# Walking a matmul's moving operand backwards, and interleaving the two token tiles of its stationary operand

## The chip, the cores and the metric

The kernel runs on one core of one Trainium2 chip. The metric is the device time of one execution in microseconds (us). The kernel before took 1279.71 us, the median of two runs (1278.69 and 1280.73). The profile is of one execution, whose span from first to last instruction is 1276.7 us.

On TensorE (PE) a matmul has two operands in SBUF. The stationary one, 128 x 128, is loaded into the array by an instruction of its own, which the profile shows on a row called PEld; the moving one is then streamed through the array column by column, up to 512 columns, and the products are summed in a bank of PSUM, 128 x 512 float32.

## The reference

A network of two blocks on 256 tokens of 1024 channels, all in float32: first a block of a state space layer and a causal attention, then two layers that each mix latent attention, a gated convolution and a retention, and end with a feed-forward network. Cut to one such feed-forward step, with the names of the kernel's weights:

```python
h = rms_norm_2(x, ln_ffn_pre)
y = (silu(h @ w_gate) * (h @ w_up)) @ w_down
x = x + rms_norm_2(y, ln_ffn_post)
```

Nearly all of the work is products of that form: 256 rows times a weight matrix of 1024 (or 2816, 512, 256, 128) rows. The change touches how these products are read and written, and nothing of what they compute.

## The kernel before

Every product with a weight matrix is done in three matmuls of a rounded float32 type (float32r in the code). An operand `a` is held as `hi + lo`, where `hi` is `a` rounded to that type and `lo` is what is left over; `x @ w` is then `xh wh + xh wl + xl wh`. The method `mm3` (lines 163 to 167) issues these three, with a block of the activations (128 channels x 128 tokens) as the stationary operand and 512 (a few times 416 or 256) columns of the weights as the moving one.

Weights arrive by `wtile` (line 142) in tiles of 256 rows x 512 columns: one DMA from SyncE's queue into a buffer `raw`, a rounding copy into `hi` on ScalarE (ACT, line 158), and a subtraction into `lo` on VectorE (DVE, line 160). `wbuf` (line 135) hands the buffers out by turns. In the state space layer `hi` and `lo` have four buffers each, in a pool `wp`; for the rest of the program each has six, four in `wp` and two in the stage's own pool `sp`, so that of each six tiles that follow each other four lie in the one place and two in the other. A tile of 2 k-blocks x 2 token tiles gives 12 matmuls.

Activations are made into stationary operands by `split` (line 186), which reads a transposed block out of PSUM (or a temporary), writes the rounded value `dh` on ACT and the remainder `dl` on DVE. `transposed` (line 196) does that for the blocks of one token tile; the pre-norms, the feed-forward, the merge, and the attention outputs all come through it or through `split`. Their pages come from `pages` (line 214): up to four channel blocks, each with its 256 tokens in a row, so that token tile `t` of a block is 128 words that follow each other:

```python
s = slice(t * 128, t * 128 + 128)
self.mm3(pts[t][:, :ncols], xh[:, s], xl[:, s], hi[:, k, :ncols], lo[:, k, :ncols], ...)
```

`gemm` (line 169) computes rows of a product for both token tiles; `out_rows` (line 241) is the last product of a block, with the residual. `gemm_t` (line 445) computes one product of the state space layer the other way round: there the weights are stationary and the activations (`s5gh`, `s5gl`) are moving. `gemm_raw` (line 421) and all attention and retention products work on plain float32.

The order of the instructions is set by a tile scheduler from the order of the code; small pieces of other work (attention heads, convolution taps on DVE) are put between the weight tiles by `pump` (line 107).

Of the kernel before, what the change touches and what calls it, by code (L numbers as in the profile page):

```python
# [23 lines left out]
C = 512  # L24
# [26 lines left out]
class Net:  # L51
# [16 lines left out]
    def stage(self, pages, temps, raws=0, halves=0):  # L68
        """pages and temporaries of a stage; what an earlier stage had is given back."""
        if getattr(self, "ctx0", None):  # L70
            self.ctx0.close()
        self.ctx0 = ExitStack()
        self.temps = temps
        self.wn, self.more = {}, {"raw": raws, "hi": halves, "lo": halves}
        self.bp = self.ctx0.enter_context(self.tc.tile_pool(name=self.nm("bp"), bufs=pages))
        self.sp = self.ctx0.enter_context(self.tc.tile_pool(name=self.nm("sp"), bufs=2))
# [8 lines left out]
    def page(self, shape, name, dt=F32):  # L85
        """up to 4 KB of each partition"""
        assert int(np.prod(shape[1:])) <= 1024, shape
        return self.bp.tile(shape, dt, tag="q4", name=self.nm(name))
# [46 lines left out]
    def wbuf(self, tag):  # L135
        """buffer of a tile of weights; the stage may have some more of them"""
        i = self.wn[tag] = self.wn.get(tag, -1) + 1
        more = self.more.get(tag, 0)
        pool, bufs = (self.wp, 4) if i % (4 + more) < 4 else (self.sp, more)
        return pool.tile([128, KT, C], F32 if tag == "raw" else F32R, tag=tag, name=self.nm(tag), bufs=bufs)  # L140
# [22 lines left out]
    def mm3(self, out, xh, xl, wh, wl, first, last):  # L163
        nc = self.nc
        nc.tensor.matmul(out, xh, wh, start=first, stop=False)  # L165
        nc.tensor.matmul(out, xh, wl, start=False, stop=False)  # L166
        nc.tensor.matmul(out, xl, wh, start=False, stop=last)  # L167

    def gemm(self, xs, W, c0, ncols, evac, pts=None):
        """rows: out[t] = x @ W[:, c0:c0+ncols]; xs: list over k blocks of (hi, lo) aps [128, 256]."""  # L170
        KB = len(xs)
        pts = [self.acc(), self.acc()]
        for k0 in range(0, KB, KT):
            kn = min(KT, KB - k0)
            hi, lo = self.wtile(W[k0 * 128:(k0 + kn) * 128, c0:c0 + ncols], kn, ncols)
            for t in range(2):
                for k in range(kn):
                    xh, xl = xs[k0 + k]
                    s = slice(t * 128, t * 128 + 128)
                    self.mm3(pts[t][:, :ncols], xh[:, s], xl[:, s], hi[:, k, :ncols], lo[:, k, :ncols],  # L180
                             k0 + k == 0, k0 + k == KB - 1)
            self.pump()
        for t in range(2):
            evac(t, pts[t][:, :ncols])

    def split(self, dh, dl, src, scale=None):
        """dh + dl = src * scale, src in PSUM."""
        nc = self.nc
        if scale is None:
            nc.scalar.activation(dh, src, AF.Copy)  # L190
            nc.vector.tensor_tensor(dl, src, dh.bitcast(F32), op=ALU.subtract)
        else:
            a = nc.scalar.activation(dh, src, AF.Copy if isinstance(scale, float) else AF.Identity, scale=scale)  # L193
            self.last_split = a, nc.vector.scalar_tensor_tensor(dl, src, scale, dh.bitcast(F32), op0=ALU.mult, op1=ALU.subtract)  # L194

    def transposed(self, t, row, pages, nb, gains=None, scale=None):
        """row [128 tok, nb*128] -> split blocks of pages, scaled per channel by gains."""
        nc = self.nc
        for b0 in range(0, nb, 4):
# [4 lines left out]
            s = slice(t * 128, t * 128 + 128)  # L204
            dh, dl = pages[b0 // 4]
            if gains is None:
                self.split(dh[:, :bn, s], dl[:, :bn, s],
                           pt[:, :bn * 128].rearrange("p (b n) -> p b n", b=bn), scale)
            else:
                for b in range(bn):  # L210
                    self.split(dh[:, b, s], dl[:, b, s], pt[:, b * 128:(b + 1) * 128],
                               gains[:, b0 + b:b0 + b + 1])

    def pages(self, nb, name="xT"):
        return [(self.page([128, min(4, nb - b), 256], name + "h", F32R), self.page([128, min(4, nb - b), 256], name + "l", F32R))
                for b in range(0, nb, 4)]

    def blocks(self, pages):
        return [(h[:, b, :], l[:, b, :]) for h, l in pages for b in range(h.shape[1])]
# [21 lines left out]
    def out_rows(self, xs, W, x, post, out=None):  # L241
        """x + rms(xs @ W) * post, or x + xs @ W when post is None; the first 128 rows are done some tiles ahead."""
# [8 lines left out]
        def product(t, n, k0, kn, hi, lo):  # L251
            s = slice(t * 128, t * 128 + 128)
            for k in range(kn):
                xh, xl = xs[k0 + k]
                self.mm3(pts[t][n], xh[:, s], xl[:, s], hi[:, k, :], lo[:, k, :], k0 + k == 0, k0 + k == KB - 1)
# [36 lines left out]
    def rsqrt1(self, v):  # L292
        """-1024 / 27 / sqrt(v) of a column, by a step of third and one of second order."""
# [16 lines left out]
    # ------------------------------------------------------------------ consts  # L310
# [25 lines left out]
    def sincos(self, out_c, out_s, ang, tag, after=None):  # L336
        """sin and cos of ang (any size that float32 reduces), ang [128, ...]"""
# [18 lines left out]
    def tables2(self):  # L356
# [8 lines left out]
        self.cs = self.sp.tile([128, 2, 2, 80], F32, tag="cs", name="cs", bufs=1)  # (cos/sin, t, mla16|ret64)  # L365
# [5 lines left out]
        # log gammas: min(x, 0) - log1p(exp(-|x|)), log1p by the atanh series  # L371
# [20 lines left out]
        # distances: [m part, mt, n]: relu(n - m), relu(m - n)  # L392
# [9 lines left out]
    # ------------------------------------------------------------------ first block: state space layer  # L402
    def raw_tiles(self, W, c0, ncols, KB):
        """sources of the tiles of gemm_raw, in its order"""
        return [W[k0 * 128:(k0 + KT) * 128, c0 + n0:c0 + n0 + C] for k0 in range(0, KB, KT) for n0 in range(0, ncols, C)]

    def load_raw(self):
        """next tile of self.todo, in any of the buffers of a tile of weights"""
# [6 lines left out]
    def gemm_raw(self, xs, ncols, evac, after=None):  # L415
        """gemm_t on float32 operands that are not split, where the tensor engine has the time: a closure for each tile of self.pre."""
# [22 lines left out]
    def gemm_t(self, xs, W, c0, ncols, evac, order=None):  # L439
        """columns: out^T = W[:, c0:c0+ncols]^T x^T, evac(block, psum [128, 256]); order of the pairs of k blocks."""  # L440
# [20 lines left out]
    def s5_params(self, after):  # L461
# [10 lines left out]
        # powers of ab: [ri, pair, k], k = 0..4  # L472
# [18 lines left out]
        # one chunk further, on (re, -im): [[a, b], [-b, a]] of ab^4  # L491
# [5 lines left out]
        # f = (ab - 1) / (lr + i li)  # L497
# [15 lines left out]
        # sums for products in three multiplications  # L513
# [4 lines left out]
    def s5_bc(self):  # L518
# [4 lines left out]
        # B~ = f B  # L523
# [20 lines left out]
    def s5_pows(self):  # L544
        """powers 1..16 of ab^4: (-im, re, im), pair, power."""
# [19 lines left out]
    def cprod(self, eng, q, l0, Z, Zx):  # L565
        """ab^l z for pairs 8q..8q+7, l = l0..l0+3, as (k1, k2, k3): re = k1 + k3, im = k1 + k2."""
# [14 lines left out]
    def s5_w(self, q, eng):  # L581
        """pairs 8q..8q+7 of ab^k B~, k = 1..4, [(g2, p), qq, (q2, k, c)], pair = 2 qq + q2, re and im."""
# [7 lines left out]
    def s5_wt(self, W, q, w, after=None):  # L590
        """their lhsT [(q2, k, c), qq, (g2, p)]"""
# [8 lines left out]
    def s5_c(self, cab, q, eng):  # L600
        """pairs 8q..8q+7 of [(g2, p), pair, (l, c')] of C ab^l, l = 0..3, re and im."""
# [4 lines left out]
    def s5(self, x_in):  # L606
# [6 lines left out]
        # normalised input; gains go on its channels after the transposes  # L613
# [6 lines left out]
        # gains go on the channels of the input; 1 / rms on what comes out of the first product and on what goes into the second  # L620
# [47 lines left out]
        # block diagonal B~ (re, -im) and the zeros before the kernel taps  # L668
# [55 lines left out]
        # chunk inputs X = W u: [(g2, p), (re, -im), pair, 1 + j], replaced by the states after each chunk  # L724
# [14 lines left out]
        # scan over the 64 chunks: inside 4 groups of 16, across the groups, then what each group takes over  # L739
# [28 lines left out]
        # kernel taps K[l] = Re(C ab^l B~): [(q4, g2, c), pg, (l, c')], channels in order; spread to lower triangles  # L768
# [19 lines left out]
        # inside a chunk  # L788
# [20 lines left out]
        gT = self.pages(8, "s5g")  # L809
# [37 lines left out]
        # gated linear unit, output  # L847
# [5 lines left out]
        def ev_glu(b, p):  # L853
# [7 lines left out]
            mh, ml = (a[:, b % 4, :] for a in mT[b // 4])  # L861
            self.split(mh, ml, m, 0.25)
# [10 lines left out]
    # ------------------------------------------------------------------ second block: mixing  # L873
    def mix(self, l, x):
# [11 lines left out]
        # ---- gates, branch outputs, merge  # L886
# [31 lines left out]
    def conv(self, l, xs, W, hf):  # L918
        """a * sigmoid(gate), taps, layer norm over channels and silu; the taps are left to run beside what follows."""
# [54 lines left out]
        def silu(b2):  # L974
# [16 lines left out]
            self.split(cT[0][0][:, 2 * b2:2 * b2 + 2, :], cT[0][1][:, 2 * b2:2 * b2 + 2, :], v)  # L991
# [8 lines left out]
    def rope_rows(self, o1, o2, x1, x2, c, s, tag):  # L1000
        """o1 = x1 c - x2 s, o2 = x2 c + x1 s"""
# [42 lines left out]
    def mla(self, l, parts):  # L1044
        """latent attention; its rows and heads are left to run beside what follows."""
# [76 lines left out]
        def out(g):  # L1122
# [11 lines left out]
            self.split(oT[0][0][:, s, :], oT[0][1][:, s, :], pt.rearrange("p (b n) -> p b n", b=2))  # L1134
# [13 lines left out]
    def retention(self, l, xs, W, rstd, half, gn):  # L1148
# [41 lines left out]
        def score(h):  # L1190
            """scores on their decay, D^T[m, n] = gamma_f^(n - m) or gamma_b^(m - n)"""
# [54 lines left out]
    # ------------------------------------------------------------------ first block: causal attention  # L1246
# [128 lines left out]
    # ------------------------------------------------------------------ ffn  # L1375
# [25 lines left out]
def _cols(a, w):  # L1401
    """[..., w*128] -> [128, n*w]: one column per block of 128 channels."""
# [68 lines left out]
```

## Time and profile before

| | |
|---|---|
| median of two runs | 1279.71 us (1278.69 to 1280.73) |
| span of the profiled execution | 1276.7 us |
| PE busy / PEld busy | 1235.7 / 1029.5 us |
| DVE busy / ACT busy | 948.3 / 652.9 us |
| read from HBM | 205.83 MB, 164 GB/s over the span |

The profile gives the profiled execution its span alone; the median of the runs is 3.0 us above it. Matmuls are pipelined: a row of the timeline gives a matmul from its start until its last result, which overlaps the next one, so the pace of TensorE is read from start to start and not from the duration. A column such as `x8` says that eight instructions were merged into one row.

### The profile page before, as it was taken

What the parts mean: (1) busy time and instruction counts of PE and PEld (TensorE: products, weight loads), DVE (VectorE), ACT (ScalarE), POOL (GpSimd) and SP (SyncE); (2) the same over time, 40 slices, a digit from 0 to 9 for tenths busy, and PEclk for the clock granted to TensorE, in tenths of its full rate; (3) what the DMA queues carried; (4) which work ended last, traced back from release to release, by engine and by line L of the source; (5) the groups of instructions that cost most, each with busy time, mean ns of one, the idle gap of its engine ahead of it and who ended that gap; (6) DMA issues with size and microseconds to landing.
All of it is one profiled execution on the core that took longest, in us unless ns stands there. A gap on an engine that the chain in (4) does not pass through costs nothing.

```text
span 1276.7 us, 17877 instructions
## 1 busy us (share of the span) xinstructions
PE 1235.7 (97%) x6520; PEld 1029.5 (81%) x6520; DVE 948.3 (74%) x1923; ACT 652.9 (51%) x1073; POOL 51.8 (4%) x42
## 2 busy tenths in 40 slices
PE   7898799999999999999999999999999999999997
PEld 6787777787888888888788887888888887888886
DVE  6999489887889998857755555899998857755544
ACT  3112467675765544544644444666545445644432
POOL 3920000000000000000000000000000000000000
PEclk9779899999999999999999999999999999999999
DMA  9326656644454554555566564544554554665661
GB/s 319 83 43 99 166 174 209 192 136 137 142 164 138 161 161 152 164 201 179 189 180 184 171 235 151 175 134 147 166 159 153 179 184 148 218 190 161 193 211 50
DMA packets 125367, 210.60 MB, mean 165 GB/s; under 512 B 22112, under 2 KB 31328, under 8 KB 125280
## 3 DMA queue, kind: packets, MB, share of 16 engines
q1 hardware_dynamic: 117056, 204.24, 50.9%
q10 hardware_dynamic: 8224, 5.23, 2.1%
q8 instruction: 51, 0.84, 0.3%
q14 instruction: 36, 0.29, 0.1%
HBM read 205.83 MB, written 3.60 MB: 164 GB/s over the span
## 4 chain that ended last, share of the span: by engine, by line
PE 79%; DVE 13%; ACT 3%; DMA 3%; issue 2%; SPq 0%; DVEq 0%; ACTq 0%
PE mm L165 23%; PE mm L167 23%; PE mm L166 22%; DVE lo L160 2%; PE sm L203 2%; ACT hi L158 1%; PE sm L1119 1%; PE sm L1211 1%; DVE cacc L957 1%; PE sm L1094 1%; DVE s5pr L745 1%; PE sm L733 1%; DVE cm L586 1%; DVE s5pr L759 1%; PE mm L455 1%
## 5 line engine op out<-in xcount | busy, mean ns | idle before, releaser
L160 DVE TENSOR_TENSOR lo<-raw,hi 128x1024 fp32r<-128x1024 f32 (+2 forms) x372 | 440.1, 1186 | 235.8 <-ACT hi L158 234.4
L158 ACT ACTIVATE hi<-raw 128x1024 fp32r<-128x1024 f32 (+2 forms) x372 | 382.6, 1032 | 377.8 <-PE mm L167 290.4
L165 PE MATMUL mm<-hi,xTh 128*128 128x512 f32 (+2 forms) x1152 | 451.1, 394 | 1.6 <-ACT xTh L193 1.5
L167 PE MATMUL mm<-hi,xTl 128*128 128x512 f32 (+2 forms) x1152 | 443.7, 386 | 0.3 <-DVE t L297 0.2
L166 PE MATMUL mm<-lo,xTh 128*128 128x512 f32 (+2 forms) x1152 | 443.3, 385 | 0.2 <-DVE lo L160 0.2
L165 PEld LDWEIGHTS mm<-hi,xTh 128*128 128x128 f32 x1152 | 216.4, 188 | 48.9 <-ACT xTh L193 7.3
L167 PEld LDWEIGHTS mm<-hi,xTl 128*128 128x128 f32 x1152 | 216.3, 188 | 46.2 <-DVE t L297 1.5
L166 PEld LDWEIGHTS mm<-lo,xTh 128*128 128x128 f32 x1152 | 216.7, 188 | 41.2 <-DVE lo L160 0.5
L957 DVE SCALAR_TENSOR_TENSOR cacc<-aT,colp,cacc 128x256 f32<-128x256 f32 x240 | 104.2, 476 | 0.0
L165 PE MATMUL mm<-hi,fh 128*128 128x512 f32 x176 | 69.0, 392 | 0.0
L166 PE MATMUL mm<-lo,fh 128*128 128x512 f32 x176 | 68.9, 392 | 0.0
L167 PE MATMUL mm<-hi,fl 128*128 128x512 f32 x176 | 68.8, 391 | 0.0
L167 PEld LDWEIGHTS mm<-hi,fl 128*128 128x128 f32 x176 | 33.0, 187 | 7.4
L165 PEld LDWEIGHTS mm<-hi,fh 128*128 128x128 f32 x176 | 33.0, 188 | 7.3
L166 PEld LDWEIGHTS mm<-lo,fh 128*128 128x128 f32 x176 | 33.0, 188 | 7.2
L277 DVE SCALAR_TENSOR_TENSOR pg<-mm,post 128x512 f32<-128x512 f32 x16 | 11.0, 690 | 21.9 <-ACT pg L275 21.9
L194 DVE SCALAR_TENSOR_TENSOR xTl<-sm,colp,xTh 128x128 fp32r<-128x128 f32 x80 | 24.3, 345 | 3.5 <-ACT xTh L193 3.1
L454 PE MATMUL mm<-s5gh,hi 128*128 128x256 f32 x64 | 19.0, 305 | 7.1 <-ACT s5gh L844 7.1
L193 ACT ACTIVATE xTh<-sm,colp 128x128 fp32r<-128x128 f32 x80 | 24.4, 381 | 1.8 <-DVE xTl L194 1.7
L895 ACT ACTIVATE pg<-mm,t 128x512 f32<-128x512 f32 x24 | 16.5, 690 | 16.9 <-PE mm L167 16.9
L733 PE MATMUL sm<-s5U,s5W 64*64 64x64 f32 x256 | 21.2, 300 | 2.5 <-DMA s5U<-s5ud 2.5
L733 PEld LDWEIGHTS sm<-s5U,s5W 64*64 64x64 f32 x256 | 20.8, 207 | 3.2 <-issue 3.2
(387 smaller groups left out, 1513.2 us busy)
## 6 DMA issues: line engine op xcount, KB each, us to landing
raw<-in_w_in SPq DMA_DIRECT2D x112, 512.0 KB, 3.5
raw<-in_ffn_w_down SPq DMA_DIRECT2D x44, 512.0 KB, 3.8
raw<-in_ffn_w_gate SPq DMA_DIRECT2D x40, 512.0 KB, 3.7
raw<-in_ffn_w_up SPq DMA_DIRECT2D x40, 512.0 KB, 3.6
raw<-in_attn_w_in SPq DMA_DIRECT2D x32, 512.0 KB, 4.3
raw<-in_ret_w_o SPq DMA_DIRECT2D x16, 512.0 KB, 3.2
raw<-in_w_out SPq DMA_DIRECT2D x16, 512.0 KB, 3.2
raw<-in_ssm_w_glu SPq DMA_DIRECT2D x8, 512.0 KB, 4.9
```

The lines of the kernel that those rows point to most:

```text
L158: nc.scalar.activation(h, r, AF.Copy)
L160: self.last_lo = nc.vector.tensor_tensor(l, r, h.bitcast(F32), op=ALU.subtract)
L165: nc.tensor.matmul(out, xh, wh, start=first, stop=False)
L166: nc.tensor.matmul(out, xh, wl, start=False, stop=False)
L167: nc.tensor.matmul(out, xl, wh, start=False, stop=last)
L193: a = nc.scalar.activation(dh, src, AF.Copy if isinstance(scale, float) else AF.Identity, scale=scale)
L194: self.last_split = a, nc.vector.scalar_tensor_tensor(dl, src, scale, dh.bitcast(F32), op0=ALU.mult, op1=ALU.subtract)
L203: nc.tensor.transpose(pt[:, b * 128:(b + 1) * 128], row[:, (b0 + b) * 128:(b0 + b + 1) * 128], self.ident)
L454: nc.tensor.matmul(o, wh, xh, start=first and b % 2 == 0, stop=False, skip_group_check=True)
L733: lx[q] = nc.tensor.matmul(pt[g * 64:g * 64 + 64, qq * 64:qq * 64 + 64], Wl[i][h][r, qq, g * 64:g * 64 + 64], U[r, 8 * h + qq, g, :], star ...
L895: nc.scalar.activation(gate[t, n], p, AF.Tanh, scale=hf(t))
L957: nc.vector.scalar_tensor_tensor(cacc[:, b, :], src, sc, cacc[:, b, :], op0=ALU.mult, op1=ALU.add)
```

## The change

`mm3` reverses the column direction of the moving operand and of the output: column 511 is streamed first and written to place 511, column 0 last. The pages that hold stationary operands are laid out as `[channel block, token within tile, token tile]` in place of `[channel block, token]`: word 0 is token 0 of tile 0, word 1 is token 0 of tile 1, and so on. A stationary operand of one token tile is therefore 128 words at a step of two words. `split` writes with the same step. The pages of `gemm_t`, whose activations are the moving operand, keep their old layout through a new method `moving`, and `gemm_t` is not reversed. No buffer is added or removed, and every instruction stays in its place on every engine; only the address patterns differ.

```diff
     def mm3(self, out, xh, xl, wh, wl, first, last):
         nc = self.nc
+        out, wh, wl = out[:, ::-1], wh[:, ::-1], wl[:, ::-1]
         nc.tensor.matmul(out, xh, wh, start=first, stop=False)
...
-                    s = slice(t * 128, t * 128 + 128)
-                    self.mm3(pts[t][:, :ncols], xh[:, s], xl[:, s], hi[:, k, :ncols], lo[:, k, :ncols],
+                    self.mm3(pts[t][:, :ncols], xh[:, t], xl[:, t], hi[:, k, :ncols], lo[:, k, :ncols],
...
-                self.split(dh[:, :bn, s], dl[:, :bn, s],
+                self.split(dh[:, :bn, t], dl[:, :bn, t],
                            pt[:, :bn * 128].rearrange("p (b n) -> p b n", b=bn), scale)
             else:
                 for b in range(bn):
-                    self.split(dh[:, b, s], dl[:, b, s], pt[:, b * 128:(b + 1) * 128],
+                    self.split(dh[:, b, t], dl[:, b, t], pt[:, b * 128:(b + 1) * 128],
...
     def pages(self, nb, name="xT"):
-        return [(self.page([128, min(4, nb - b), 256], name + "h", F32R), self.page([128, min(4, nb - b), 256], name + "l", F32R))
-                for b in range(0, nb, 4)]
+
+        return [(self.stationary(min(4, nb - b), name + "h"), self.stationary(min(4, nb - b), name + "l")) for b in range(0, nb, 4)]
+
+    def stationary(self, nb, name):
+
+        return self.page([128, nb, 128, 2], name, F32R).rearrange("p b n t -> p b t n")
+
+    def moving(self, nb, name):
+
+        return [tuple(self.page([128, min(4, nb - b), 256], name + p, F32R) for p in "hl") for b in range(0, nb, 4)]
...
-                self.mm3(pts[t][n], xh[:, s], xl[:, s], hi[:, k, :], lo[:, k, :], k0 + k == 0, k0 + k == KB - 1)
+                self.mm3(pts[t][n], xh[:, t], xl[:, t], hi[:, k, :], lo[:, k, :], k0 + k == 0, k0 + k == KB - 1)
...
-        gT = self.pages(8, "s5g")
+        gT = self.moving(8, "s5g")
...
-            mh, ml = (a[:, b % 4, :] for a in mT[b // 4])
-            self.split(mh, ml, m, 0.25)
+            self.split(*(a[:, b % 4] for a in mT[b // 4]), m.rearrange("p (t n) -> p t n", t=2), 0.25)
...
-            self.split(cT[0][0][:, 2 * b2:2 * b2 + 2, :], cT[0][1][:, 2 * b2:2 * b2 + 2, :], v)
+            self.split(*(a[:, 2 * b2:2 * b2 + 2] for a in cT[0]), v.rearrange("p b (t n) -> p b t n", t=2))
...
-            self.split(oT[0][0][:, s, :], oT[0][1][:, s, :], pt.rearrange("p (b n) -> p b n", b=2))
+            self.split(oT[0][0][:, s], oT[0][1][:, s], pt.rearrange("p (b t n) -> p b t n", b=2, t=2))
```

## Rows read from the trace of the kernel before

**Rows 1.** The page's first part (busy time, share of the span, instructions), the slices of PE and of the granted clock of TensorE (a digit is a tenth of full, 40 slices of 31.9 us), and the chain that ended last by engine and by line.

```profile
span 1276.7 us, 17877 instructions
PE 1235.7 (97%) x6520; PEld 1029.5 (81%) x6520; DVE 948.3 (74%) x1923; ACT 652.9 (51%) x1073; POOL 51.8 (4%) x42
...
PE   7898799999999999999999999999999999999997
...
PEclk9779899999999999999999999999999999999999
...
PE 79%; DVE 13%; ACT 3%; DMA 3%; issue 2%; SPq 0%; DVEq 0%; ACTq 0%
PE mm L165 23%; PE mm L167 23%; PE mm L166 22%; DVE lo L160 2%; PE sm L203 2%; ACT hi L158 1%; PE sm L1119 1%; PE sm L1211 1%; DVE cacc L957 1%; PE sm L1094 1%; DVE s5pr L745 1%; PE sm L733 1%; DVE cm L586 1%; DVE s5pr L759 1%; PE mm L455 1%
```

**Rows 2.** The groups of matmuls of line 165, the first of the three of `mm3`, by shape (lines 166 and 167 have as many each): out <- moving, stationary; array rows x columns; shape; count; busy us, mean ns of one; idle time before.

```profile
L165 PE MATMUL mm<-hi,xTh 128*128 128x512 f32 x1056 | 421.9, 401 | 1.1 <-ACT xTh L193 1.0
L165 PE MATMUL mm<-hi,fh 128*128 128x512 f32 x176 | 69.0, 392 | 0.0
L165 PE MATMUL mm<-hi,xTh 128*128 128x256 f32 x64 | 18.1, 284 | 0.0
L165 PE MATMUL mm<-hi,oTh 128*128 128x512 f32 x32 | 13.1, 410 | 0.0
L165 PE MATMUL mm<-hi,s5mh 128*128 128x512 f32 x32 | 12.8, 403 | 0.1
L165 PE MATMUL mm<-hi,cTh 128*128 128x512 f32 x32 | 12.7, 397 | 0.0
L165 PE MATMUL mm<-hi,xTh 128*128 128x416 f32 x32 | 11.6, 380 | 0.6 <-ACT xTh L193 0.5
L165 PE MATMUL mm<-hi,mcTh 128*128 128x512 f32 x16 | 6.3, 391 | 0.0
L165 PE MATMUL mm<-hi,mcTh 128*128 128x256 f32 x8 | 2.2, 279 | 0.0
```

**Rows 3.** The timeline of PE in a steady stretch of the first feed-forward's last product: start us, us, engine, line, operation, tiles, shape, count. From the first row to the last there are 48 steps from start to start, four tiles of weights.

```profile
762.23 0.39 PE L165 MATMUL mm<-hi,fh 128*128 128x512 f32 x1
762.45 0.40 PE L166 MATMUL mm<-lo,fh 128*128 128x512 f32 x1
...
773.12 0.39 PE L165 MATMUL mm<-hi,fh 128*128 128x512 f32 x1
```

**Rows 4.** The same timeline, the stretch right after it, the next two tiles of weights: 23 steps from the first row to the last.

```profile
773.36 0.39 PE L166 MATMUL mm<-lo,fh 128*128 128x512 f32 x1
...
778.73 0.39 PE L165 MATMUL mm<-hi,fh 128*128 128x512 f32 x1
```

**Rows 5.** The chain that ended last, in order of time (start us, us on the chain, what): plain float32 matmuls of 256 columns (line 1211) and of 64 columns (line 1119).

```profile
476.83 1.73 PE sm L1211 x8
...
881.11 0.84 PE sm L1119 x8
...
882.87 0.84 PE sm L1119 x8
```

**Rows 6.** The timeline of PE in `gemm_t` (rounded type, 256 columns, activations moving), at its start; 20 steps from the first row to the last.

```profile
141.20 0.41 PE L455 MATMUL mm<-s5gl,hi 128*128 128x256 f32 x1
...
145.47 0.41 PE L456 MATMUL mm<-s5gh,lo 128*128 128x256 f32 x1
```

**Rows 7.** The same, later in `gemm_t`; 30 steps from the first row to the last.

```profile
149.80 0.28 PE L455 MATMUL mm<-s5gl,hi 128*128 128x256 f32 x1
...
153.40 0.28 PE L455 MATMUL mm<-s5gl,hi 128*128 128x256 f32 x1
```

**Rows 8.** The busy time by stretch: from:to us, length, PE busy (count), granted clock of TensorE as a share of full, DMA share, GB/s.

```profile
141.20:145.40 4.20, 4.20 (x21) 0.50 0.88 252
149.80:153.40 3.60, 3.60 (x33) 1.00 0.56 196
...
762.20:773.00 10.80, 10.80 (x49) 1.00 0.58 196
773.10:778.70 5.60, 5.60 (x25) 1.00 0.51 152
```

**Rows 9.** The timeline of the weight loads (PEld) in the stretch of rows 3.

```profile
762.23 0.19 PEld L166 LDWEIGHTS mm<-lo,fh 128*128 128x128 f32 x1
762.45 0.19 PEld L167 LDWEIGHTS mm<-hi,fl 128*128 128x128 f32 x1
```

**Rows 10.** Groups of instructions by line and shape on ACT and DVE (columns as in rows 2): the rounding copy and the subtraction of the state space layer, which write at a step of four words (lines 844 and 845), a pass of ACT over the same shape without a step (line 839), and the splits.

```profile
L844 ACT ACTIVATE s5gh<-s5gf 128x512 fp32r<-128x512 f32 x4 | 4.5, 1126 | 0.1
L839 ACT ACTIVATE s5gf<-pg 128x512 f32<-128x512 f32 x4 | 2.5, 627 | 9.6 <-DMA pg<-s5yd 9.6
L845 DVE TENSOR_TENSOR s5gl<-s5gf,s5gh 128x512 fp32r<-128x512 f32 x4 | 4.5, 1128 | 9.5 <-ACT s5gh L844 9.5
L191 DVE TENSOR_TENSOR fl<-sm,fh 128x512 fp32r<-128x512 f32 x20 | 12.8, 682 | 0.0
L193 ACT ACTIVATE xTh<-sm,colp 128x128 fp32r<-128x128 f32 x80 | 24.4, 381 | 1.8 <-DVE xTl L194 1.7
```

**Rows 11.** Busy time by stretch of the two convolutions' neighbourhood: length, then PE, PEld, DVE, ACT, POOL busy (count), granted clock, DMA share, GB/s.

```profile
850.00:950.00 100.00, 100.00 (x513) 83.88 (x512) 95.39 (x184) 57.27 (x96) 0.00 (x0) 1.00 0.49 151
300.00:450.00 150.00, 149.58 (x780) 125.35 (x779) 128.68 (x305) 92.77 (x189) 0.00 (x0) 1.00 0.47 147
```

More of the change, by code (lines that the diff above doesn't have):

```diff
@@ L203, in transposed @@
                 nc.tensor.transpose(pt[:, b * 128:(b + 1) * 128], row[:, (b0 + b) * 128:(b0 + b + 1) * 128], self.ident)
-            s = slice(t * 128, t * 128 + 128)
             dh, dl = pages[b0 // 4]
             if gains is None:
-                self.split(dh[:, :bn, s], dl[:, :bn, s],
+                self.split(dh[:, :bn, t], dl[:, :bn, t],
                            pt[:, :bn * 128].rearrange("p (b n) -> p b n", b=bn), scale)
@@ L210, in transposed @@
                 for b in range(bn):
-                    self.split(dh[:, b, s], dl[:, b, s], pt[:, b * 128:(b + 1) * 128],
+                    self.split(dh[:, b, t], dl[:, b, t], pt[:, b * 128:(b + 1) * 128],
                                gains[:, b0 + b:b0 + b + 1])
     def pages(self, nb, name="xT"):
-        return [(self.page([128, min(4, nb - b), 256], name + "h", F32R), self.page([128, min(4, nb - b), 256], name + "l", F32R))
-                for b in range(0, nb, 4)]
+        return [(self.stationary(min(4, nb - b), name + "h"), self.stationary(min(4, nb - b), name + "l")) for b in range(0, nb, 4)]
[3 more added lines that the diff above has]
+        return [tuple(self.page([128, min(4, nb - b), 256], name + p, F32R) for p in "hl") for b in range(0, nb, 4)]
     def blocks(self, pages):
-        return [(h[:, b, :], l[:, b, :]) for h, l in pages for b in range(h.shape[1])]
+        return [(h[:, b], l[:, b]) for h, l in pages for b in range(h.shape[1])]
     def prenorm(self, x, gains):
@@ L251, in product @@
         def product(t, n, k0, kn, hi, lo):
-            s = slice(t * 128, t * 128 + 128)
             for k in range(kn):
                 xh, xl = xs[k0 + k]
-                self.mm3(pts[t][n], xh[:, s], xl[:, s], hi[:, k, :], lo[:, k, :], k0 + k == 0, k0 + k == KB - 1)
+                self.mm3(pts[t][n], xh[:, t], xl[:, t], hi[:, k, :], lo[:, k, :], k0 + k == 0, k0 + k == KB - 1)
         tiles = [(k0, n) for k0 in range(0, KB, KT) for n in range(2)]
```

## The prediction

> **What bounds the kernel now.** I read the page first: TensorE is busy for 1235.7 of 1276.7 us, and the chain that ended last runs on PE for 79% of the span, 68% of it (23 + 23 + 22) in the three matmuls of `mm3`; the granted clock is full from about the sixth slice on [rows 1]. So what one `mm3` matmul takes from start to start is nearly what the kernel takes. Next, how many there are: line 165 issues 1056 + 176 + 32 + 32 + 32 + 16 = 1344 of 512 columns, 32 of 416 and 72 of 256 [rows 2]; with lines 166 and 167 that is 4032, 96 and 216.
>
> Then their pace, from the timeline. In one stretch 48 steps take 773.12 - 762.23 = 10.89 us, 227 ns each [rows 3]; in the next, 23 steps take 5.37 us, 233.5 ns each [rows 4]. Both lie at the full clock of 2.4 GHz [rows 8], where 512 columns need 213.3 ns at one column per cycle. The fast stretch is four tiles of weights long, the slow one two, as the buffers `wp` and `sp` take turns: the same instruction on the same shapes runs 6.5 ns apart by the place of its operand. Mean of 4 and 2: 229.2 ns.
>
> Three more views say what the excess over 213.3 ns is.
> - Plain float32 matmuls of 256 columns, at the same clock, step by 1.73 us / 8 = 216 ns [rows 5]. 216 is 512 cycles and 2.7 ns, so these take two cycles for a column. With twice the time for each word of the moving operand the excess is nearly gone.
> - `gemm_t`, in the rounded type, steps by 4.27 us / 20 = 213.5 ns for 256 columns [rows 6] at half clock, 1.2 GHz [rows 8], which is 256 cycles and nothing more. At full clock the same matmuls step by 3.60 us / 30 = 120 ns [rows 7, 8], where 256 cycles are 106.7: excess 13.3.
> - So the excess is 13.3 ns for 256 columns and 13.7 to 20.2 for 512. It goes by the matmul rather than by the column, and shows only when the moving operand is read at full pace. What happens once per matmul at a fixed size is the load of the next stationary operand, 128 columns, which begins with each matmul (762.23, 762.45) and lasts 0.19 us [rows 3, 9].
>
> I read this as the two reads of SBUF, moving and stationary, getting in each other's way, more or less by their relative place. No row shows it directly.
>
> **The change part by part.** No instruction, DMA, wait or buffer is added, removed or moved on any queue. Three address patterns differ.
>
> (a) *Moving operand backwards, stationary at a step of two words.* The moving read goes at 4 bytes per 0.417 ns, 9.6 bytes/ns. The pace of a load is bounded by the 64-column matmuls, which cost no more than 128 cycles = 53 ns of streaming and yet step by 0.84 / 8 = 105 ns [rows 5], so they go at the pace of the loads: 4 bytes per 0.82 ns, 4.9 bytes/ns. With a step of two words the load walks at 9.8, the pace of the moving read, and the two run opposite ways. Today one overtakes the other at two to one, and they meet in every phase; with equal pace their relation is fixed by the start and could stay clear. The gain is bounded below by zero, above by an excess that falls from 229.2 to the 216 of the plain matmuls: 13.2 ns x 4032 = 53.2 us. I take the upper end, because excess differs by place already now [rows 3, 4] and is absent where the pace is lower [rows 5, 6]: relative place and pace, which the change alters, are what it hangs on. In the chain the three lines hold 68% of 1276.7 = 868 us, that is 868 / 0.2292 = 3787 matmuls; 3787 x 13.2 ns = **50.0 us**.
>
> (b) *What takes over.* From 850 to 950 us DVE is already busy 95.39 of 100 us [rows 11]. There a faster TensorE runs into the taps of the convolution and the subtractions of line 160: 68% of 100 us / 0.2292 = 297 matmuls, 3.9 us, which I take as lost. From 300 to 450 DVE is at 128.68 / 150 = 86% [rows 11] and would come to about 91%; nothing taken off. **Minus 4.**
>
> (c) *The splits write at a step of two words.* No row has that step. Above: a step of four words costs ACT 1126 against 627 ns for 512 elements, and DVE 1128 against 682 [rows 10], 0.97 and 0.87 ns an element. The splits that TensorE waits for are the pre-norms', 80 of 128 elements on each engine; 80 x 128 x 0.97 = 10 us if ACT's are all on the path (its wait for them is now 1.0 us [rows 2]). Below: nothing, or a little gained, as no reason forbids it. I take **minus 2**: most lie beside `out_rows`' late tiles, and two words is nearer to no step than to four. If that cover goes, TensorE waits at the start of each of the five pre-norms.
>
> [...] No row before has a strided load.
>
> (d) *Matmuls of 416 and 256 columns*, 312 of them: at most 13 ns each, 4 us; taken as zero, kept for the lower end.
>
> Sum: 50.0 - 4 - 2 = 44 us. Against the profiled execution 1276.7 - 44 = 1232.7; the median is 3.0 us above that span, so **1236 us**. If only half of the excess goes: 1279.7 - 22 = 1258. If all of it goes everywhere: 1279.7 - 53.2 - 4 = 1223. The likeliest case's own range is 1223 to 1258.
>
> **The rivals.**
>
> *No change: the excess is a fixed cost of the rounded type.* 227 ns is 545 cycles, 17 for each 16 columns; a read that pauses so at any layout would be untouched. For it: the steady 227 over 48 matmuls [rows 3]. Against: 13.3 ns at 256 columns, twice as much per column as at 512 [rows 7], and the 6.5 ns by place [rows 4]. If only the slow third came down to 227: 1344 x 6.5 ns = 9 us; if all were slow: 2688 x 6.5 = 17 us more. 1271 to 1297, likeliest 1280. [...]
>
> *Slower: the load takes twice as much from the stream.* A stationary operand at a step of two words spans 1024 bytes in place of 512. If the excess is paid by the stretch of memory that the load touches, and not by place or direction, it doubles: 4032 x 13.2 = 53 us more, **1333 us**. This decides if the excess of a step comes to 26 ns, 242 ns a step; already 6.4 ns more for each of 4032 is over 2%. For it: the excess goes by the matmul and not by the column [rows 3, 7], and a step of four words nearly doubles a pass of ACT and DVE [rows 10]. Against: two phases of the same load differ by half of the excess [rows 3, 4], which a price by length would not show.
>
> *Slower by far: a descending stream runs at half pace.* If TensorE reads or writes single words when going backwards, a step is 512 columns at 0.833 ns, 427 ns, as at half clock [rows 6]: 4032 x 198 ns = 798 us more, about 2080. No row has a negative step, so neither excludes it. [...]
>
> **How the numbers follow.** Two per cent, 26 us, is about what a measurement of this kernel can tell from no change. Chances: the excess goes, wholly or mostly, 0.58; no change, with the pieces of the first case that gain under 26 us, 0.22; slower 0.20, of which the doubled load has 0.15 and half pace 0.05. The first case and the second hold 0.80 together, so the range reaches from 1223 to 1290; it takes in 10 us for the splits.
>
> **What the changed profile would show.** Right: in the stretches of rows 3 and 4 steps near 216 ns, `gemm_t` still at 120, plain matmuls at 216, DVE over 97% from 850 to 950, the split rows of lines 190 to 194 within some 10% of today's. The doubled load would show steps of 235 to 245 ns at unchanged clock; half pace, steps near 427. The prediction is wrong if the step stays at 227 and 233, or if the pace of 216 comes but the waits of line 158 and of the pre-norms' line 193 eat it.

## The result and the profile after

The changed kernel takes 1293.02 us (median of two runs, 1292.42 and 1293.62) against 1279.71: a ratio of 1.0105, with a 95% interval of 1.0076 to 1.0134. It is 13.3 us slower, where a gain of 44 was forecast, and above the range of 1223 to 1290. That is less than the two per cent which the prediction took as about what a measurement can tell from no change, but the interval leaves 1 out: the loss is small and real.

The page of the changed kernel, as in [rows 1]: span, busy time, the granted clock in 40 slices, and the chain that ended last by engine. `mm3` is now lines 166 to 168.

```profile
span 1291.4 us, 17871 instructions
PE 1248.1 (97%) x6520; PEld 1060.1 (82%) x6520; DVE 949.6 (74%) x1923; ACT 656.7 (51%) x1073; POOL 42.9 (3%) x42
...
PEclk9798899999999999999999999999999999999999
...
PE 83%; DVE 10%; ACT 3%; DMA 2%; issue 1%; SPq 0%; ACTq 0%; DVEq 0%
```

The span grew by 14.7 us, PE's busy time by 12.4, and the counts of instructions on PE, PEld, DVE and ACT are as before. PE's share of the chain rose from 79% to 83%: nothing else became the bound, TensorE itself is slower. The timeline of PE in the changed kernel, the same 48 and 23 steps as [rows 3] and [rows 4]:

```profile
770.12 0.40 PE L166 MATMUL mm<-hi,fh 128*128 128x512 f32 x1
...
781.32 0.40 PE L166 MATMUL mm<-hi,fh 128*128 128x512 f32 x1
781.56 0.40 PE L167 MATMUL mm<-lo,fh 128*128 128x512 f32 x1
...
786.92 0.40 PE L166 MATMUL mm<-hi,fh 128*128 128x512 f32 x1
```

11.20 us / 48 = 233.3 ns where it was 227, and 5.36 / 23 = 233.0 where it was 233.5 (over 23 steps the rows' hundredths of a us are worth 0.4 ns each, so these two are the same). The tiles in `wp`, which had the better pace, lost it; those in `sp` kept theirs. The clock is not the reason. Busy time by stretch (columns as in [rows 11]), the two stretches above, granted clock 1.00 in both:

```profile
770.12:781.32 11.20, 11.20 (x49) 9.46 (x48) 4.90 (x4) 4.25 (x4) 0.00 (x0) 1.00 0.58 189
781.56:786.92 5.36, 5.36 (x24) 4.46 (x23) 2.45 (x2) 2.08 (x2) 0.00 (x0) 1.00 0.55 159
```

The size fits. With four tiles of six in `wp`, a step rose by 6.3 x 4/6 = 4.2 ns on the mean; with the 3787 steps that the prediction counted on the chain that is 16 us, against 14.7 in the span. The whole trace says the same: where two matmuls of 512 columns follow each other without a wait (steps under 260 ns), the mean step was 228.0 ns for weights in `wp` and 233.3 for those in `sp`, and is now 233.9 and 233.3; 2524 such steps in `wp` at 5.9 ns more are 15 us. So the loss is the pace of the 512-column matmuls, and the question is what sets it.

### The profile page after: what moved, and what is told of

It reads as the page before. It is cut to its first block, busy times and chain, and to the rows that moved or that the text cites. A ratio compares the mean times of both kernels' runs of the same rounds, so it can differ in the third digit from the quotient of the medians.

```text
span 1291.4 us, 17871 instructions
## 1 busy us (share of the span) xinstructions
PE 1248.1 (97%) x6520; PEld 1060.1 (82%) x6520; DVE 949.6 (74%) x1923; ACT 656.7 (51%) x1073; POOL 42.9 (3%) x42
## 4 chain that ended last, share of the span: by engine, by line
PE 83%; DVE 10%; ACT 3%; DMA 2%; issue 1%; SPq 0%; ACTq 0%; DVEq 0%
PE mm L166 24%; PE mm L167 24%; PE mm L168 24%; PE sm L203 2%; DVE s5pr L751 1%; PE sm L1124 1%; PE sm L1099 1%; PE sm L1216 1%; DVE lo L160 1%; ACT hi L158 1%; DVE s5X L756 1%; DVE cm L592 1%; DVE s5pr L765 1%; PE mm L461 1%; DVE cm L580 1%
## 5 line engine op out<-in xcount | busy, mean ns | idle before, releaser
L166 PE MATMUL mm<-hi,xTh 128*128 128x512 f32 (+2 forms) x1152 | 457.5, 399 | 1.6 <-ACT xTh L193 1.4
L168 PE MATMUL mm<-hi,xTl 128*128 128x512 f32 (+2 forms) x1152 | 450.1, 392 | 0.2
L167 PE MATMUL mm<-lo,xTh 128*128 128x512 f32 (+2 forms) x1152 | 449.9, 391 | 0.1
L166 PEld LDWEIGHTS mm<-hi,xTh 128*128 128x128 f32 x1152 | 225.7, 196 | 44.5 <-ACT xTh L193 6.6
L168 PEld LDWEIGHTS mm<-hi,xTl 128*128 128x128 f32 x1152 | 225.7, 196 | 41.2 <-DVE t L303 1.4
L167 PEld LDWEIGHTS mm<-lo,xTh 128*128 128x128 f32 x1152 | 225.8, 196 | 37.1 <-DVE lo L160 0.5
L1394 ACT ACTIVATE pg<-mm,t 128x512 f32<-128x512 f32 (+1 forms) x24 | 15.6, 652 | 14.9 <-PE mm L168 14.9
L281 ACT ACTIVATE pg<-mm 128x512 f32<-128x512 f32 x16 | 9.5, 596 | 26.6 <-PE mm L168 26.6
```

The lines of the kernel that those rows point to most:

```text
L1394: nc.scalar.activation(sg[t][:, :nn], p, AF.Silu, scale=rstd[:, t:t + 1])
```

## Experiments

Two kinds were run: the kernel before, or the changed one, with one edit, and microbenchmarks that do nothing of the network but blocks of 36 matmuls with nothing else beside them, at a granted clock of 1.00, each run once. Ratios are to the kernel before as it ran beside the edited one (medians 1277.80 us for the first three such edits, 1279.08 for the last two). In a timeline of a microbenchmark a block is one row (start us, us, line, tiles, shape, count); its step is its length less that of its last matmul (0.39 or 0.40 us at 512 columns, 0.38 at 496, 0.335 at 384), divided by 35. Steps below are from the trace's own start times, which the two decimals of a row give to 0.3 ns. Digits at the end of a block's name are not shown. "Distance" below is the address of the stationary operand less that of the moving one within a partition.

**One pattern at a time, by itself.**

`mov` and `sta` are of the rounded type; `m0` and `s0` count words of 4 bytes.

```diff
+    def block(name, n=512, rev_m=False, rev_o=False, m0=0, step=1, s0=0, cols=128, reps=REPS):
+        p = ps.tile([128, 512], F32, tag="bank", name=name, bufs=4)
+        for i in range(reps):
+            a = m0 + 512 * (i % 3)
+            m = mov[:, a:a + n]
+            b = s0 + 128 * step * (i % 4)
+            s = sta[:, b:b + step * cols:step] if step > 1 else sta[:, b:b + cols]
+            o = p[:cols, :n]
+            if rev_m:
+                m = m[:, ::-1]
+            if rev_o:
+                o = o[:, ::-1]
+            nc.tensor.matmul(o, s, m, start=i == 0, stop=i == reps - 1)
+        return p
```

> A kernel that does no part of the network: 18 blocks of 36 matmuls of the rounded type right after one another, 512 columns and a contiguous stationary operand of 128 columns unless a block's name says otherwise, each block with one thing changed; its output is not the network's. Read from it: steps from start to start. All theories: base 227 (moving operand at a multiple of 128 bytes). Theory 'length' (the load takes from the stream by the bytes it walks over): step2 and step2rev 240, step4 above that; revboth, revmov, revout 227; cols64 220, cols32 217. Theory 'phase' (the relative place and pace of two reads sets it): step2 233 whichever way the stream runs, movat64 233, movat32 and movat16 in between, staat64 233, bothat64 227 again; cols64 and cols32 between 213 and 227. Theory 'direction' (a descending stream costs): revmov or revout 233, revboth 233, step2 227. Theory 'fixed' (17 cycles for 16 columns whatever the load): cols64, cols32 227, n384 170, n256 113.

The timeline of PE of this run; in order: plain; both moving operand and output reversed; moving alone; output alone; stationary at a step of two words; that and both reversed; a step of four; then, after the blocks with the moving operand 64, 32 and 16 bytes on, which are left out here, the stationary 64 bytes on; both operands 64 bytes on; loads of 64 columns; loads of 32 columns.

```profile
22.57 8.32 PE L40 MATMUL base<-mov,sta 128*128 128x512 f32 x36
30.73 8.57 PE L40 MATMUL revboth<-mov,sta 128*128 128x512 f32 x36
39.13 8.56 PE L40 MATMUL revmov<-mov,sta 128*128 128x512 f32 x36
47.53 8.34 PE L40 MATMUL revout<-mov,sta 128*128 128x512 f32 x36
55.71 8.56 PE L40 MATMUL step<-mov,sta 128*128 128x512 f32 x36
64.11 8.57 PE L40 MATMUL step2rev<-mov,sta 128*128 128x512 f32 x36
72.51 8.62 PE L40 MATMUL step<-mov,sta 128*128 128x512 f32 x36
...
105.95 8.57 PE L40 MATMUL staat<-mov,sta 128*128 128x512 f32 x36
114.36 8.34 PE L40 MATMUL bothat<-mov,sta 128*128 128x512 f32 x36
122.54 8.45 PE L40 MATMUL cols<-mov,sta 128*64 128x512 f32 x36
130.83 8.51 PE L40 MATMUL cols<-mov,sta 128*32 128x512 f32 x36
```

The plain block steps at (8.32 - 0.39) / 35 = 226.6 ns (226.7 by the start times), the output reversed at 227.1. The moving operand reversed, or the stationary one at a step of two, or both, come to 233.3 to 233.4: each is enough, and they do not add. A step of four gives 234.9. Moving the stationary operand alone by 64 bytes costs the same, 233.6, and moving both by 64 gives it back (227.2). The moving operand alone, moved by 64, 32 and 16 bytes, gives 228.8, 233.1 and 231.9. None of the four theories came through whole: "phase" had the first of these three at 233, "length" had the step of two at 240 and "direction" at 227, where it came to 233.3, and "fixed" had a block of 256 columns at 113, which came to 119.6. So the two paces of the kernel before, 227 and 233, are there with no other engine at work, and hang on how far apart the operands lie.

The last two blocks load fewer columns: groups of weight loads (out <- operands, array rows x columns, shape, count | busy us, mean ns of one | idle).

```profile
L40 PEld LDWEIGHTS base<-mov,sta 128*128 128x128 f32 x36 | 6.8, 188 | 1.4
...
L40 PEld LDWEIGHTS cols<-mov,sta 128*64 128x64 f32 x36 | 4.8, 134 | 3.4
L40 PEld LDWEIGHTS cols<-mov,sta 128*32 128x32 f32 x36 | 3.9, 109 | 4.4
```

With a load of 134 ns the step is 230.1, with 109 it is 231.9: a shorter load buys nothing, it costs 3 to 5 ns, where the theories that spoke of it had expected 227 or less. So the excess over 213.3 ns (512 columns at the 0.417 ns that one column adds, by the blocks of other lengths below) is not a price for each column that the load reads. Every matmul of these blocks still has a load, so a cost that comes with a load of any length is not excluded.

**One half of the change in the kernel.** First the reversal alone, added to the kernel before; then the interleaved pages alone, the changed kernel less its reversal.

```diff
     def mm3(self, out, xh, xl, wh, wl, first, last):
         nc = self.nc
+        out, wh, wl = out[:, ::-1], wh[:, ::-1], wl[:, ::-1]
```

> Only the reversal of the moving operand and of the output is made; stationary pages stay contiguous. Theory 'direction': the whole loss, ratio 1.009 to 1.012, steps of 233 in every stretch. Theories 'length' and 'phase' (by the step of two words): within 0.3% of the kernel before, the two stretches at 227 and 233 as before.

```diff
     def mm3(self, out, xh, xl, wh, wl, first, last):
         nc = self.nc
-        out, wh, wl = out[:, ::-1], wh[:, ::-1], wl[:, ::-1]
```

> Only the stationary pages are interleaved; the stream runs forward. Theories 'length' and 'phase': the whole loss, ratio 1.009 to 1.012, all steps at 233 and weight loads of 196 ns in place of 188. 'Length' would also let the slow third go to 240, which the changed kernel's profile already speaks against. Theory 'direction': ratio within 0.3% of 1.

1290.66 us, ratio 1.0105 (1.0089 to 1.0120), and 1290.60 us, ratio 1.0093 (1.0078 to 1.0109). Each half loses about what the whole change loses, where each theory had one of them lose and the other within 0.3%. The timeline of PE with the reversal alone, the stretches of [rows 3] and [rows 4]:

```profile
767.35 0.40 PE L166 MATMUL mm<-hi,fh 128*128 128x512 f32 x1
...
778.54 0.40 PE L166 MATMUL mm<-hi,fh 128*128 128x512 f32 x1
778.78 0.40 PE L167 MATMUL mm<-lo,fh 128*128 128x512 f32 x1
...
784.14 0.40 PE L166 MATMUL mm<-hi,fh 128*128 128x512 f32 x1
```

and with the interleaved pages alone:

```profile
768.75 0.39 PE L165 MATMUL mm<-hi,fh 128*128 128x512 f32 x1
...
779.94 0.39 PE L165 MATMUL mm<-hi,fh 128*128 128x512 f32 x1
780.17 0.40 PE L166 MATMUL mm<-lo,fh 128*128 128x512 f32 x1
...
785.54 0.39 PE L165 MATMUL mm<-hi,fh 128*128 128x512 f32 x1
```

11.19 / 48 = 233.1 ns in both for `wp`, 5.36 / 23 = 233.0 and 5.37 / 23 = 233.5 for `sp`.

**Only the place, in the kernel.** If the pace hangs on place, the kernel before can be made faster, and can be made as slow as the changed one, without touching a pattern. By the addresses in the compiled program, the distance modulo 512 is 0 for all weights in `wp` (2700 of the 4032 matmuls of 512 columns) and 320 for all in `sp` (1332). Two small tiles, each in the pool of another stage, are made 64 bytes larger, so that `sp`'s buffers move on by 64 bytes and the distance becomes 256:

```diff
-        rsum = self.sp.tile([128, 2, 8], F32, tag="m_sum", name=self.nm("a_sum"), bufs=1)
+        rsum = self.sp.tile([128, 2, 16], F32, tag="m_sum", name=self.nm("a_sum"), bufs=1)[:, :, :8]
...
-        rsum = self.sp.tile([128, 2, 8], F32, tag="m_sum", name=self.nm("m_sum"), bufs=1)
+        rsum = self.sp.tile([128, 2, 16], F32, tag="m_sum", name=self.nm("m_sum"), bufs=1)[:, :, :8]
```

> The kernel before with one small tile of the stage's pool made 64 bytes longer, so that the two extra buffers of weights in that pool begin at a multiple of 128 bytes as those of the first pool do. Theory 'phase': the slow third falls from 233 to 227, 1344 matmuls x 6.5 ns = 8.7 us at most, of which 68 to 94% on the chain: ratio 0.993 to 0.996. Theory 'length' and 'direction' say nothing of it; if the pool itself (how far apart the operands lie) and not the 64 bytes sets the pace: ratio 1.000.

1271.75 us, ratio 0.9949 (0.9937 to 0.9962): faster than both kernels. The timeline, same stretches:

```profile
758.85 0.39 PE L165 MATMUL mm<-hi,fh 128*128 128x512 f32 x1
...
769.73 0.39 PE L165 MATMUL mm<-hi,fh 128*128 128x512 f32 x1
769.95 0.39 PE L166 MATMUL mm<-lo,fh 128*128 128x512 f32 x1
...
775.16 0.39 PE L165 MATMUL mm<-hi,fh 128*128 128x512 f32 x1
```

10.88 / 48 = 226.7 and now 5.21 / 23 = 226.5: the slow third has the pace of the others (227.6 in both places over the whole trace). The same edit in the changed kernel:

> The changed kernel with the extra buffers of weights moved to a multiple of 128 bytes, as in the run that did so to the kernel before. If a pattern of two words or a reversed stream pins the pace at 233 whatever the place: ratio to the kernel before 1.008 to 1.013, as the changed kernel itself. If place still counts: 1.003 to 1.007.

1294.98 us, ratio 1.0121 (1.0105 to 1.0136): no gain. The same stretches:

```profile
771.49 0.40 PE L166 MATMUL mm<-hi,fh 128*128 128x512 f32 x1
...
782.68 0.40 PE L166 MATMUL mm<-hi,fh 128*128 128x512 f32 x1
782.92 0.40 PE L167 MATMUL mm<-lo,fh 128*128 128x512 f32 x1
...
788.28 0.40 PE L166 MATMUL mm<-hi,fh 128*128 128x512 f32 x1
```

11.19 / 48 = 233.1 and 5.36 / 23 = 233.0, as without the edit. With the patterns of the change this move of `sp`, which helped the kernel before, no longer matters. The opposite edit in the kernel before, its patterns untouched, moves the weights in `wp` on by 64 bytes and the stationary pages and `sp` by 128, which makes the distance 64 modulo 256 for all tiles:

```diff
+        self.cp.tile([128, 16], F32, name="shift")
+        self.xp.tile([128, 16], F32, tag="back", name="back", bufs=1)
```

> The kernel before, contiguous and forward as it was, with every buffer of split weights (those of the first pool too) 64 bytes off a multiple of 128, the stationary pages where they were. If the change lost its time by the pace of 233 alone, and by nothing else it does: all stretches at 233, 2688 matmuls x 6.5 ns = 17 us at most, ratio 1.007 to 1.013, as the changed kernel. If the loss has another source beside the pace: ratio clearly lower than the changed kernel's 1.0105.

1291.25 us, ratio 1.0093 (1.0076 to 1.0110), and in the timeline:

```profile
768.52 0.39 PE L167 MATMUL mm<-hi,fh 128*128 128x512 f32 x1
...
779.72 0.39 PE L167 MATMUL mm<-hi,fh 128*128 128x512 f32 x1
779.96 0.39 PE L168 MATMUL mm<-lo,fh 128*128 128x512 f32 x1
...
785.32 0.39 PE L167 MATMUL mm<-hi,fh 128*128 128x512 f32 x1
```

11.20 / 48 = 233.3, 5.36 / 23 = 233.0 (233.3 in both places over the whole trace). A shift of 64 bytes, with no pattern changed, costs about what the whole change costs.

**What the fixed part is.** The same blocks at other lengths, other types and other distances. Here and in the next run one call of a kind is shown, and the comments, which the code does not have, name the others.

```diff
+    block("na496", n=496)            # and 480, 448, 320
+    block("nb512", n=512, s0=16)     # 64 bytes apart; and 448, 384, 320, 256
+    block("bf16", kind="b")
+    block("plain256", n=256, kind="f")
+    block("rev64", rev_m=True, s0=16)     # and 32 bytes apart, and 256 columns
+    block("step2at64", step=2, s0=16)     # and a step of three, and 256 columns
+    block("sta32", s0=8)
+    block("sta128", s0=32)
```

> A second kernel that does no part of the network: blocks of 36 matmuls, contiguous and 512 columns unless named; na: both operands at a multiple of 128 bytes, nb: the stationary operand 64 bytes off; its output is not the network's. Theory 'fixed gap' (each matmul of the rounded type costs 32 cycles more than its columns when both lie alike and 48 when they lie 64 bytes apart): na496 220, na480 213, na448 200, na320 147; nb512 233, nb448 207, nb384 180, nb320 153, nb256 127. Theory 'lock' (17 cycles for 16 columns, then rounded up to the next multiple of 32 cycles, shifted by 16 when the operands lie 64 bytes apart): na496 227, na480 213, na448 200, na320 147; nb512 233, nb448 207, nb384 180, nb320 153, nb256 113. Both: bf16 216 (half the bytes for each column), plain256 216. A reversed stream that is slow only by its place: rev64 227, rev32 between; slow by itself: rev64 and rev32 at 231 or more. rev256 and step2n256 120. step2at64 and step3 233 or more, sta128 227.

Four of its rows: 496 columns at distance 0; 384 columns at distance 64; bfloat16, 512 columns; plain float32.

```profile
31.00 8.08 PE L43 MATMUL na<-mov,sta 128*128 128x496 f32 x36
...
74.98 6.40 PE L43 MATMUL nb<-mov,sta 128*128 128x384 f32 x36
90.75 7.94 PE L43 MATMUL bf<-movb,stab 128*128 128x512 bf16 x35
98.53 15.70 PE L43 MATMUL plain<-x 128*128 128x256 f32 x72
```

The views give the clock as a share and not as a frequency, so a cycle here is the time that a column adds at a granted clock of 1.00: 320 columns step at 146.7 ns and 512 at 226.7, both at distance 0, which is 80.0 / 192 = 0.417 ns, or 2.4 columns per ns, the rate that the prediction writes as 2.4 GHz at one column per cycle. At a granted clock of 0.50 `gemm_t` takes 213.5 / 256 = 0.834 ns for a column [rows 6, 8], twice that. 496 columns step at 220.0 ns, 528 cycles: 32 more than columns, as 512 has (544). 384 columns at distance 64 step at 173.3, 416 cycles: again 32, and no loss by place (173.6 at distance 0 in the first run), where 512 columns at the same distance take 560 (233.3 ns). 320 columns take 352 cycles (146.7 ns) at both distances, 448 columns 486 (38 more). 480 columns at distance 0 take 40 more, 256 columns 31 at distance 0 and 27 at 64. So the cost above one cycle per column is 27 to 40 cycles per matmul, 32 at four of these seven lengths, and 48 only for 512 columns at a bad place; of the five lengths tried at both distances, 512 alone lost by place. Neither theory's numbers for the shorter blocks at distance 64 held. In bfloat16 the 36 steps to the next block's start take 98.53 - 90.75 = 7.78 us, 216 ns each (one of the 36 records is missing), and plain float32 of 256 columns steps at 216 as in [rows 5] (72 rows for 36 matmuls: each makes two), with a load of 190 ns, as long as the rounded type's 188. So a load as long does not by itself bring the excess. But both these types read the moving operand at about half the bytes per ns, 512 columns of 2 bytes or 256 of 4 in 216 ns (4.7 bytes per ns) where the rounded type reads 512 of 4 in 226.7 (9.0), so the runs do not tell a cost of the rounded type from one that comes with reading at the full pace. Two more expectations failed: a distance of 128 bytes, expected fast, came to 232.4, and a step of two words at distance 64, expected at 233 or more, to 230.1 (a step of three, at distance 0, 235.7).

**Is there any place at which the changed patterns are fast?**

```diff
+    block("sta192", s0=48)           # and 256, 320, 384, 448, 4 bytes
+    block("rev4", rev_m=True, m0=1)  # and distances of 128, 192, 256, 384
+    block("step128", step=2, s0=32)  # and 192, 256, 384
+    block("sr128", step=2, s0=32, rev_m=True)
```

> This run computes no part of the network: blocks of 36 matmuls of the rounded type, 512 columns, as in the first two microbenchmarks; only the place of the stationary operand (bytes past its place in the first block), the direction of the moving one and the step of the stationary one differ. Theory 'likeness modulo 256 bytes': forward and without a step, the stationary operand 256 bytes on steps at 227 ns as the first block does; 4, 192, 320, 384 and 448 bytes on at 232 to 234. Rival 'slow only within 128 bytes of the place, or fast only at 0': 192 or 320 and 384 at 227, or 256 at 233. For the changed kernel's two patterns: theory 'phase', by which the reversed stream and the interleaved load only stand at a bad place: among the reversed blocks (moving operand 4 bytes on; stationary 128, 192, 256, 384 bytes on) and the interleaved ones (128, 192, 256, 384 on) at least one comes to 227. Rival 'pattern': a reversed stream, or a load at a step of two words, has no place at which it is fast, and all of these stay at 232 to 235.

Timelines of single blocks: the plain pattern at distances 256 and 320, reversed at 256, a step of two words at 256.

```profile
40.59 8.32 PE L43 MATMUL sta<-mov,sta 128*128 128x512 f32 x36
48.75 8.56 PE L43 MATMUL sta<-mov,sta 128*128 128x512 f32 x36
...
107.40 8.57 PE L43 MATMUL rev<-mov,sta 128*128 128x512 f32 x36
...
140.94 8.56 PE L43 MATMUL step<-mov,sta 128*128 128x512 f32 x36
```

All distances tried with the plain pattern, in ns per step: 

| distance modulo 512 | 0 | 4 | 32 | 64 | 128 | 192 | 256 | 320 | 384 | 448 |
|---|---|---|---|---|---|---|---|---|---|---|
| step, ns | 226.7 | 232.2 | 233.1 | 233.3 | 232.4 | 229.0 | 226.7 | 233.4 | 232.4 | 229.1 |

The second half repeats the first: the pace goes by the distance modulo 256, and of those tried only 0 is fast. The blocks of the first run with the moving operand moved fit in as distances 448, 480 and 496 (228.8, 233.1, 231.9). 192 and 448 had been expected at 232 or more and lie between. Reversed, no distance of seven tried (0, 32, 64, 128, 192, 256, 384) is below 233.3 (at 64 without one longer step of 420 ns). A reversed stream begins at its last word, 4 bytes below the place of a forward one modulo 256, and a distance of 4 is slow by the table; so one block moves the moving operand 4 bytes on, and it is at 235.5: that is not the reason. At a step of two words 0, 64, 128, 192, 256 and 384 give 230.1 to 233.3, and both patterns at 128 give 233.3. The theory "phase", which I held until this run, falls: the patterns do not merely stand at a bad place, they have no place at 227 among those tried.

## Why the prediction was wrong

**What bounds the kernel** was right. TensorE's pace in `mm3` is nearly the time: 6.3 ns on the tiles in `wp` moved the span by 14.7 us, and back in the other direction 64 bytes of padding gave 6 us.

**The excess.** The views were read rightly (227 and 233 by place, 216 for plain float32, 13.3 at 256 columns), and so was the sentence that place decides between 227 and 233. What failed is the step from there to the cause: "what happens once per matmul at a fixed size is the load", so the whole excess is two reads in each other's way and a better relation of the two can take it off. 227 - 216 = 11 ns of it is there at the best place, in every direction and step tried, and does not fall with a shorter load (steps of 230.1 and 231.9 ns with loads of 134 and 109); only the last 6.7 ns go by place. That these 11 ns are gone in bfloat16 (216 ns), in plain float32 (216) and at half clock (213.5 ns for 256 columns, twice 106.7) [rows 6] does not say that a slower stream frees the load; a fixed cost of one type at one clock would look the same there. Which of the two it is stays open.

**(a), the term of 50.0 us, is the step that failed**, twice over. Its upper end was 13.2 ns a step, of which no run got more than the 2.5 from the mean of 229.2 to the best place's 226.7; and its argument, that equal paces fix the relation of the two walks "and could stay clear", held no reason for the good end over the bad one. Measured, each pattern alone puts every tile at 233 ns: +4.2 ns a step in place of -13.2. The bound "below by zero" was the graver fault: the trace held a slower pace of the same instruction [rows 4], and 2688 steps that could fall to it.

**(b)** never came into play. **(c)** was right in size: the splits of lines 193 and 194 went from 381 to 391 ns on ACT and from a median of 344 to 346 on DVE, 160 passes at 10 ns or less, under the 2 us taken. ACT's larger splits rose by a little over a tenth (line 190, `xTh`, 512 elements, from a median of 588 ns to 651), a little more than the sign "within some 10%" allowed; ACT's share of the chain stayed at 3%.

```profile
L193 ACT ACTIVATE xTh<-sm,colp 128x128 fp32r<-128x128 f32 x80 | 24.7, 391 | 1.8 <-DVE xTl L194 1.7
```

**(d)** holds: the matmuls of 416 columns in `mm3` step at a median of 189 ns before and after, those of 256 columns at 120, and a block of 256 columns steps at 119.6 plain, 118.3 reversed and 120.1 at a step of two. `gemm_t` (line 439 of the kernel before, 445 of the changed one), untouched, makes the 30 steps between these two rows of its timeline in 3.60 us, 120 ns each.

```profile
148.31 0.28 PE L460 MATMUL mm<-s5gh,hi 128*128 128x256 f32 x1
...
151.91 0.28 PE L460 MATMUL mm<-s5gh,hi 128*128 128x256 f32 x1
```

**The rivals.** *No change* was nearest: the runs show a cost per matmul of the rounded type that no layout tried took off (whether it is the type's own stays open, as said), and its clause "if all were slow: 2688 x 6.5 = 17 us more" is what happened (13.3). I had it as the far edge of a rival, at 1297, and then cut the range at 1290. The objection that I held against it, twice as much per column at 256 as at 512, speaks only against the form I gave it (17 cycles for each 16 columns), not against a fixed cost per matmul: 32 cycles are 13.3 ns at either length. *The load takes twice as much* fell: a step of two words lengthens the load from 188 ns to between 193 and 197, and steps are 233, not 242. *Half pace* fell: 233, not 427, and a reversed output costs nothing (227.1 against 226.7).

A matmul of 512 columns steps at 216 ns in the bfloat16 block and at 226.7 to 233.6, 544 to 560 cycles, in the rounded type, contiguous and forward. From the rows of plain float32 I had taken 216 as within reach for it. Whether the load takes time from a running matmul is not shown either way: the shorter loads, which bought nothing (230.1 and 231.9 ns against 226.6), speak against it, and that 64 bytes between the operands cost 6.7 ns (233.4 against 226.7) speaks for it.

## What to carry to other kernels

When the same instruction runs at two paces in one trace, compare the addresses of its operands before giving the difference a cause, and count first what is lost if all fall to the slower pace: here that clause held the result. For matmuls of the rounded type with 512 columns, these runs say: let moving and stationary operands start at the same place modulo 256 bytes, read both forward and without a step: 64 bytes of padding in two small tiles gave 0.5% here, and 64 bytes the other way cost 0.9%. A floor taken from one number type (216 ns) is no floor for another until a block of that type alone has been seen at it.

## What the hardware showed that was not expected

- A matmul of the rounded type takes 32 cycles of 0.417 ns more than its columns at 512, 496, 384 and 320 columns (226.7, 220.0, 173.6 and 146.7 ns), at the full granted clock and the best place; 480 and 448 come to 40 and 38. Why 32, whether the type or the load or the full pace of reading brings it, and why it grows to 48 for 512 columns at a bad place and not for 448, 384 or 320, is not known from these runs.
- The pace of 512 columns depends on the distance of the operands modulo 256 bytes, from 226.7 to 233.6 ns, with nothing else running.
- A moving operand read backwards (233.3 to 235.5 ns), and a stationary one at a step of two words (230.1 to 233.3), each bring the slow pace at every place tried, and together no more than one of them (233.3 to 233.4). What in the reads does this stays open.
- Of a reversed moving operand with its output reversed too, only the moving side costs (233.3 alone, 233.4 with the output, 227.1 for the output alone).
